# Attention of a hybrid decoder: eight heads per token tile, probabilities turned by VectorE in 32 by 32 blocks, values in 32-row products

## The chip, the cores and the metric

One NeuronCore of a Trainium2 chip, one launch of one program. The metric is the device time of the launch in microseconds. A run is timed several times; the profile is one further execution with its own time.

The engines are named as in the profile: PE is TensorE's matrix products and PEld its loading of weights, DVE is VectorE, ACT is ScalarE, POOL is GpSimd, SP is SyncE, which here only issues DMAs. In the code they are `T`, `V`, `A`, `G` and `nc.sync`.

## The reference

Two layers (DEPTH = 2) over 1024 tokens of width 1024, all in f32. A layer normalises x, modulates it, projects it to 3088 columns, runs three groups of heads beside each other, gates each and projects back:

```python
h = rms_norm(x, pre_gain) * (1.0 + scale) + shift
(aq, ak, av, ag, rq, rk, rv, rg, gq, gk, gv, gg, ga) = jnp.split(h @ w_in, IN_SPLITS, axis=-1)
a_out = sliding_window_attention(rotary(aq), rotary(ak), av, sinks) * silu(ag)   # 8 heads on 2 kv heads, width 64
r_out = rms_norm(retention(rotary(rq), rotary(rk), rv)) * silu(rg)               # 4 heads
g_out = rms_norm(gated_linear_attention(gq, gk, gv, log_a)) * silu(gg)           # GLA, 4 heads
y = concat([a_out, r_out, g_out]) @ w_out
x = x + gate * rms_norm(y, post_gain)
```

The change concerns the attention. Each of the eight token tiles of 128 tokens looks at itself and at the tile before it: key j of the two tiles is allowed for query i where 0 <= i + 128 - j < 128. So of the previous tile the keys after the query's own place are allowed, of the current tile those up to it: exactly 128 keys for each query, which together fill one 128 by 128 square. Four query heads share one key and value head. A learned sink per head adds one logit to the softmax, whose probability is dropped:

```python
s = einsum('bnqhgd,bnkhd->bnhgqk', qb, kk) * D ** -0.5          # kk: previous and current tile
s = where(valid, s, -1e30)
p = softmax(concatenate([s, sink], -1), -1)[..., :-1]
o = einsum('bnhgqk,bnkhd->bnqhgd', p, vv)
```

## The kernel before, in words

**Stages.** A layer (`layer`) runs: modulation and the normalised, transposed input; the projection of the gates of GLA and retention; retention; GLA (`do_gqk`, `do_gv`, job `gla_core`); keys and values of the attention (`do_kv`); its queries (`attn_rot`); the projection of the attention's gates (`project_T` with `ag0`, `ag1`, job `gate`); the output projection. In layer 1 the output projection forms sums and differences of token pairs first (`last_output`, `sw_first`, the input `w_last`). A projection product of f32 is made of three passes over a split into a high and a low part (`PASSES`, `split`), 24 products of 128 by 128 weights with 256 or 512 moving columns each; all products of `mult` stand at L165, all transposes of TensorE at L180, all copies of the helper `copy` at L149 (ACT) or beside it, all DMAs of the helper `dma` at L154.

**The order of PE.** PE's instructions run in the order in which the program emits them (`tc.manual_schedule` for PE alone). A planner writes this order while the program is built: `clk` adds up an assumed cost of every product; a job is a generator that emits some work and yields either a latency from the table `L` (`lat("aq3", l)`) or the name of a flag; `pump()` between two pieces of a projection resumes every job whose time has come, so its products stand between those of the projection. `await_flag` moves the clock forward to a flag. The other engines, and SP's DMA queue, are ordered by the framework around that. The table `EN` says which engine makes each copy or DMA.

**Memory.** PSUM has eight banks: three under `mm()` for the projections, five under `aux()` for everything else. SBUF tiles come from rotating tags: `t2` (512 columns, B2 = 10), `t1` (256 columns, B1 = 8), `smx` for the softmax (SMB = 3), `mx` (`mix_tile`) for mixed inputs of the output projection, which the attention uses for its queries as well.

**Attention.** `attn_kv(l, t, pk)` copies the values of a token tile to SBUF (tag `va`, eight of them), turns the keys by rotary and transposes them into `kT`, high and low. `attn_rot(l, hf, g, w_)` projects the queries of half hf (four token tiles) and head group g (four heads) transposed, so that head channels lie on partitions, applies rotary with tables loaded from DRAM (`tabS`), swaps row blocks by small DMAs (`qst`), and a job (`split_later`, L839) splits them into high and low. `attn_run` goes over halves, groups, token tiles and starts one job `attn_q` for each: 32 units over both layers. A unit of four heads:

- scores: twelve products (two pairs of heads, three passes, two row halves side by side) into two aux banks;
- out of PSUM into `smx` 128 x 4 x 129: the previous tile's scores by ACT (`sprev`), over them the current tile's allowed ones by DVE's masked copy (L920, mask `curmask`); the 129th column is the sink;
- softmax: maximum on DVE (L922), four exponentials with sums on ACT (L925), reciprocal on DVE (L928), scaling on POOL (L929);
- after the latency `aq3`: four transposes on PE (L180) into one aux bank, copied to SBUF by ACT (`pf0`); POOL keeps the causal part in a second tile `pr` (affine_select);
- after `aq4`: the values as two products over 128 keys, once all keys with the previous tile's values, once the causal part with the difference `vd = v[t] - v[t-1]` (POOL), each in two column halves, into one aux bank; ACT copies it out (`aoc`), a DMA stores it to `aoS` in DRAM.

`gate(g, hf, kk, pm)` waits for the flags of the four `attn_q` of its half and group, loads their rows from `aoS`, multiplies them by the gate (L1590 on DVE), splits and stores the result to `mixS` (layer 1: some to `mixF`). The output projection loads `mixS` by `load_mix`.

Emission order around it: `do_kv(0)`, `do_gv(3)`, `do_kv(1..3)`, `job(attn_run)`, then `attn_rot` for the two halves and two groups, then the gates of half 0 and half 1, then the output.

Other lines that the text names: L1099, L1120 and L1121 are in GLA (`gla_core`), L635 in the normalisation (`rstd_of`), L1248 in `finish`, L533 and L515 to L545 in the weight loader (`loader`, `convert`), L704 and L666 in `pre`.

## Time and profile before

| | us |
|---|---|
| median of 3 runs | 998.84 |
| lowest and highest | 996.67, 999.44 |
| the profiled execution, its own time | 996.31 |
| its span in the profile | 994.6 |

| engine | busy us | share of the span | instructions |
|---|---|---|---|
| PE | 965.7 | 97% | 7133 |
| DVE | 683.2 | 69% | 1679 |
| ACT | 409.3 | 41% | 1152 |
| POOL | 246.3 | 25% | 310 |

The mean granted TensorE clock of this execution is 0.991 of full speed. The profiled execution lies 2.5 us under the median and 0.4 us under the lowest of the timed runs.

How to read it: a row of groups names the line, the engine, the operation, output <- inputs with the tile names of the program, partitions x elements, the count, busy time and mean ns of one instruction, and behind the last bar the idle time of the engine just before them and what ended most of it. A row of a timeline has the start in us from the span's start, the duration, the engine and the operation; products that follow one another are one row. PE's products overlap, so a row's duration exceeds the distance to the next start. A chain row names what released the step after it.

### The profile page before, as it was taken

To read this page: it belongs to the slowest core of one execution; us is meant where nothing else is said; L and a number is where in the kernel's file an instruction comes from. 1 tells how busy PE (TensorE), PEld (TensorE's weight loads), DVE (VectorE), ACT (ScalarE), POOL (GpSimd) and SP (SyncE) were. 2 spreads that over 40 slices of the span, in tenths; PEclk is the share of its full clock that TensorE was granted. 3 is DMA by queue.
4 is the path that set the end of the run, shared out by engine and by line. 5 is a ranking of instruction groups with operands and counts; after the bars stand their busy time and mean duration, and the time that the engine had idled before them with its cause. 6 is when DMAs were issued, how large, how long until landed. Compare 5 with 4: busy or idle time off the path is not lost.

```text
span 994.6 us, 19641 instructions
## 1 busy us (share of the span) xinstructions
PE 965.7 (97%) x7133; PEld 824.3 (83%) x7133; DVE 683.2 (69%) x1679; ACT 409.3 (41%) x1152; POOL 246.3 (25%) x310
## 2 busy tenths in 40 slices
PE   5899999999999999999999999999999999999996
PEld 1599999888998777778889999988999877777785
DVE  3779857677766777664677286775766577567876
ACT  2477312233332656632555332133333257574222
POOL 2322001233310234420124101113322034545000
PEclk8899999999999999999999999999999999999999
DMA  9843513523135355587555241352122434378883
GB/s 321 290 138 97 159 44 115 177 86 121 61 100 166 91 157 168 170 274 239 189 170 171 69 150 38 118 157 83 53 93 86 127 91 133 112 235 266 267 262 139
DMA packets 112305, 148.77 MB, mean 150 GB/s; under 512 B 12065, under 2 KB 63821, under 8 KB 112209
## 3 DMA queue, kind: packets, MB, share of 16 engines
q1 hardware_dynamic: 106512, 137.96, 44.5%
q10 hardware_dynamic: 5696, 9.56, 2.6%
q8 instruction: 56, 0.92, 0.4%
q14 instruction: 41, 0.33, 0.1%
HBM read 109.20 MB, written 36.18 MB: 146 GB/s over the span
## 4 chain that ended last, share of the span: by engine, by line
PE 80%; DVE 7%; DMA 7%; issue 2%; POOL 1%; ACT 1%; SPq 0%; ACTq 0%; POOLq 0%; DVEq 0%
PE mm L165 61%; PE aux L165 14%; PE aux L180 5%; DMA st<-in_w_in_dram 2%; POOL sm L635 1%; DMA t<-aoS 1%; DMA st<-in_w_last_dram 1%; DMA xk<-in_x_dram 1%; DVE arena L533 1%; DMA a<-mixS 1%; DVE t L1248 0%; DVE t L328 0%; DMA t<-in_x_dram 0%; DMA t<-xs 0%; DMA mixS<-t 0%
## 5 line engine op out<-in xcount | busy, mean ns | idle before, releaser
L165 PE MATMUL mm<-arena 128*128 128x256 f32 (+2 forms) x1824 | 299.9, 318 | 1.8 <-ACT arena L704 1.8
L165 PE MATMUL mm<-arena,arena 128*128 128x256 f32 (+2 forms) x1824 | 298.2, 316 | 0.0
L165 PEld LDWEIGHTS mm<-arena 128*128 128x128 f32 x1824 | 255.5, 191 | 26.0 <-issue 3.3
L165 PEld LDWEIGHTS mm<-arena,arena 128*128 128x128 f32 x1824 | 252.2, 188 | 24.3 <-issue 3.7
L635 POOL TENSOR_TENSOR sm<-sm,mhalf 128x1 f32<-128x1 f32 (+1 forms) x64 | 55.8, 872 | 335.9 <-DVE sm L634 317.8
L165 PE MATMUL mm<-arena,mx 128*128 128x512 f32 (+1 forms) x564 | 130.6, 387 | 0.5 <-ACT kept L1341 0.5
L165 PEld LDWEIGHTS mm<-arena,mx 128*128 128x128 f32 x564 | 101.4, 188 | 24.7 <-issue 1.9
L149 ACT ACTIVATE t<-aux 128x256 f32<-128x256 f32 (+2 forms) x124 | 55.8, 468 | 73.8 <-PE aux L180 62.2
L149 ACT ACTIVATE arena<-st 128x512 fp32r<-128x512 f32 x94 | 56.2, 627 | 53.2 <-DMA st<-in_w_in_dram 19.4
L929 POOL TENSOR_TENSOR smx<-smx,sm 128x512 f32<-128x512 f32 x32 | 36.1, 1129 | 125.7 <-DVE sm L928 118.0
L533 POOL TENSOR_TENSOR arena<-st,arena 128x512 fp32r<-128x512 f32 x31 | 42.7, 1378 | 79.7 <-ACT arena L149 72.9
L533 DVE TENSOR_TENSOR arena<-st,arena 128x512 fp32r<-128x512 f32 x77 | 58.0, 775 | 5.2 <-ACT arena L149 3.3
L925 ACT ACTIVATE smx<-smx,sm 128x129 f32<-128x129 f32 x128 | 49.9, 393 | 25.9 <-DVE sm L922 25.7
L364 DVE SCALAR_TENSOR_TENSOR acc<-st,c_act,acc 128x512 f32<-128x512 f32 x60 | 46.7, 778 | 16.9 <-DMA st<-in_w_mod_dram 16.5
L180 PE MATMUL aux<-c_ident,t 128*128 128x128 f32 (+1 forms) x292 | 48.2, 282 | 5.4 <-DVE t L666 5.0
L180 PEld LDWEIGHTS aux<-c_ident,t 128*128 128x128 f32 (+1 forms) x292 | 35.0, 144 | 12.4 <-DVE t L666 6.9
L698 ACT ACTIVATE t<-aux,mod,mod 128x128 f32<-128x128 f32 x68 | 25.9, 459 | 43.0 <-DVE t L1248 18.1
L165 PEld LDWEIGHTS aux<-t,mx 32*128 32x128 f32 (+1 forms) x896 | 39.5, 187 | 3.9 <-issue 2.1
L973 ACT ACTIVATE t<-aux 128x256 f32<-128x256 f32 x32 | 12.3, 383 | 73.6 <-PE aux L165 65.0
L165 PE MATMUL aux<-t,mx 32*128 32x32 f32 (+1 forms) x896 | 40.7, 272 | 0.0
L920 DVE COPY_PREDICATED smx<-c_curmask,aux 128x256 f32<-128x256 int32 x64 | 25.4, 446 | 19.5 <-ACT smx L149 17.2
L1248 DVE SCALAR_TENSOR_TENSOR t<-t,sm,t 128x512 f32<-128x512 f32 x32 | 24.0, 780 | 18.2 <-DMA t<-in_x_dram 10.8
(224 smaller groups left out, 1387.7 us busy)
## 6 DMA issues: line engine op xcount, KB each, us to landing
st<-in_w_in_dram SPq DMA_DIRECT2D x96, 256.0 KB, 3.8
st<-in_w_mod_dram SPq DMA_DIRECT2D x64, 256.0 KB, 3.1
mx<-mixS SPq DMA_DIRECT2D x20, 512.0 KB, 4.9
mixS<-t SPq DMA_DIRECT2D x72, 128.0 KB, 3.7
st<-in_w_last_dram SPq DMA_DIRECT2D x36, 256.0 KB, 3.8
wm<-in_w_mod_dram SPq DMA_DIRECT2D x12, 512.0 KB, 7.0
t<-in_x_dram SPq DMA_DIRECT2D x24, 256.0 KB, 4.9
t<-tabS SPq DMA_DIRECT2D x16, 256.0 KB, 4.6
```

Source lines behind the costliest of these rows:

```text
L149: A.activation(dst, src, AF.Copy)
L165: T.matmul(dst, lhsT, rhs, start=start, stop=stop)
L180: T.transpose(dst, src, idn)
L364: V.scalar_tensor_tensor(acc, wt, c_act[:, k:k + 1], acc, ALU.mult, ALU.add)
L533: e.tensor_tensor(lo, st, f(hi), ALU.subtract)
L635: G.tensor_tensor(r, r, mhalf[:, :w], ALU.pow)
L698: A.activation(hf[:, ks], at[kt], AF.Identity, scale=gain, bias=shift)
L920: V.copy_predicated(sv, curmask.unsqueeze(1).to_broadcast((P, 2, P)), pv[:, :, n // P - 1, :])
L925: A.activation(sm[:, h, :], sm[:, h, :], AF.Exp, bias=mx[:, h:h + 1], accum_out=sums[:, h:h + 1])
L929: eng("pn").tensor_tensor(sm[:, :, 0:128], sm[:, :, 0:128], rs.unsqueeze(2).to_broadcast((P, 4, P)), ALU.mult)
L973: A.activation(sq, po, AF.Square)
L1248: V.scalar_tensor_tensor(xt[j], yg[j], r, xt[j], ALU.mult, ALU.add)
```

## The change

Attention is computed per token tile for all eight heads, in 16 units instead of 32.

- **Queries.** `attn_rot` keeps both groups of a half in one f32 `mx` tile; `attn_q` splits the 128 tokens it needs (`qs`, one buffer). The `tabS` loads are issued only after the copy of a given value tile (`kv["at"]`). `attn_rot` of half 0 and `job(attn_run)` now stand ahead of `do_kv(2)` and `do_kv(3)`.
- **Scores.** 24 products into four aux banks; four `sprev` copies and four masked copies; the softmax works on 128 x 8 x 129; POOL scales 128 x 8 x 128.
- **The turn.** No transposes on PE, no PSUM copy of them, no affine_select. DVE transposes the scaled probabilities in place in 32 by 32 blocks: block (i, j) of queries and keys stays in its place and is turned inside. So a partition block i of 32 rows then holds, for every key block j, the 32 keys of j on its partitions and the 32 queries of i as columns.
- **The causal part.** Only the diagonal blocks are mixed between the two tiles: `pr`, four POOL products of 32 partitions with a 32 by 32 mask (`dmask`).
- **Values.** They go to DRAM (`vS`), and `attn_v(p)` loads them for a pair of tiles with each 32-key block replicated on the four partition blocks (five DMAs). For partition block i and round s, key block (i + s) mod 4 uses the current tile's values below the diagonal and the previous tile's elsewhere; a last round adds `pr` with `vd`. That makes 40 products with 32 rows, 64 columns and 128 moving columns (20 for token tile 0), into four aux banks, one per partition block i. The copies out of them alternate between ACT (`aoc0`) and DVE (`aoc1`); one DMA stores the tile to `aoS`.
- **Order.** `attn_run` starts a unit only after the scores of the unit before (flag `sc`) and, from the fourth on, after the values three units back (flag `av`); `load_mix` waits for the scores of single tiles. Latencies: `aq1` 11, `aq2` 2.6, `aq4` 17, `aq6` 7.
- **Memory.** B1 = 7 instead of 8; `smx` tiles are twice as wide; the eight `va` tiles are gone; the scratch for dynamic DMAs is set to 1024.

The diff, cut to its core:

```diff
-    def split_later(mq, q, name):
...
     def attn_kv(l, t, pk):
         kr = t1()[:, 0:P]
-        v = kv["v"]
-        v[t] = gp.tile([P, P], F32, tag="va", name=nm("va"), bufs=VDB)
-        A.activation(v[t], pk[:, 128:256], AF.Copy)
+        v = t1()[:, 0:P]
+        i = A.activation(v, pk[:, 128:256], AF.Copy)
+        if t in (2, 6):
+            kv["at"] = i
+        dma("sv", vS[t], v)
...
+    def attn_v(p):
+
+        x = gp.tile([P, 10, P], F32, tag="vx", name=nm("vx"), bufs=2)
+        for i in range(4):
+            dma("lv", x[32 * i:32 * i + 32, 0:8], vS[2 * p:2 * p + 2].rearrange("t (j b) d -> b (t j) d", b=32))
+        dma("lv", x[:, 8:10], vS[2 * p:2 * p + 2].rearrange("t k d -> k t d"))
+        kv[("v", p)] = x
 
     def attn_run(l):
...
+        yield (0.0, ("kT", l, 3))
+        attn_v(0)
+        attn_v(1)
+        for t in range(NT):
+            yield (lat("aq1", l) if t else 0.0, ("q", l, t // 4, 1))
+            yield (0.0, ("kT", l, t))
+            if t:
+                yield (0.0, ("sc", l, t - 1))
+            if t >= SMB:
+                yield (0.0, ("av", l, t - SMB))
+            job(attn_q(l, t, kv[t // 4]))
+
+    def attn_q(l, t, q):
+
+        qs = gp.tile([P, 2, 4, P], F32R, tag="qs", name=nm("qs"), bufs=1)
+        split(qs[:, 0], qs[:, 1], q[:, :, P * (t % 4):P * (t % 4) + P])
+        sm = gp.tile([P, 8, 129], F32, tag="smx", name=nm("smx"), bufs=SMB)
...
+        yield lat("aq2", l)
+        pss = [[aux(), aux()], [aux(), aux()]]
...
-        eng("pn").tensor_tensor(sm[:, :, 0:128], sm[:, :, 0:128], rs.unsqueeze(2).to_broadcast((P, 4, P)), ALU.mult)
-        yield lat("aq3", l)
-
-        pp = aux()
-        for h in range(4):
-            transp(pp[:, h * P:(h + 1) * P], sm[:, h, 0:128], ident)
-        pf = t2()
-        copy("pf0", pf, pp)
...
+        ph = sm[:, :, 0:128]
+        eng("pn").tensor_tensor(ph, ph, rs.unsqueeze(2).to_broadcast((P, 8, P)), ALU.mult)
+        pb = ph.rearrange("p h (j b) -> p h j b", j=4)
+        V.transpose(pb, pb)
+        cur, prev = kv[("v", t // 2)], kv.get(("v", max(t - 1, 0) // 2))
+        tc_, tp = t % 2, (t - 1) % 2
         if t > 0:
-            pr = t2()
-            G.affine_select(h4(pr), h4(pf), [[0, 4], [1, P]], ALU.is_ge, 0.0, base=0, channel_multiplier=-1)
-            parts.append((vd, pr))
+            vd = gp.tile([P, P], F32, tag="vd", name=nm("vd"), bufs=1)
+            G.tensor_tensor(vd, cur[:, 8 + tc_], prev[:, 8 + tp], ALU.subtract)
+            pr = gp.tile([P, 8, 32], F32, tag="pr", name=nm("pr"), bufs=1)
+            for i in range(4):
+                rr = slice(32 * i, 32 * i + 32)
+                eng(f"pr{i}").tensor_tensor(pr[rr], pb[rr, :, i, :], dmask[rr].unsqueeze(1).to_broadcast((32, 8, 32)),
+                                            ALU.mult)
         yield lat("aq4", l)
-        po = aux()
...
+        po = [aux() for _ in range(4)]
+        for s in range(5 if t else 4):
+            for i in range(4):
+                rr = slice(32 * i, 32 * i + 32)
+                j = (i + s) % 4
+                if t == 0 and j > i:
+                    continue
+                for r in range(2):
+                    cc = slice(64 * r, 64 * r + 64)
+                    d3 = po[i][cc, 0:128].rearrange("p (h a) -> p h a", h=4)
+                    if s == 4:
+                        w_, x = vd[rr, cc], pr[rr, r:8:2, :]
+                    else:
+                        w_ = cur[rr, 4 * tc_ + j, cc] if j < i or t == 0 else prev[rr, 4 * tp + j, cc]
+                        x = pb[rr, r:8:2, j, :]
+                    mult(d3, w_, x, s == 0, s == (4 if t else -i % 4 if i < 2 else 3), 0.03)
+        ao = t2()
+        av = ao.rearrange("p (h q) -> p h q", h=4)
+        for i in range(4):
+            copy(f"aoc{i % 2}", av[:, :, 32 * i:32 * i + 32], po[i][:, 0:128].rearrange("p (h a) -> p h a", h=4))
+        flag(("av", l, t))
+        dma("sao", aoS[t], av)
...
+        if t in (2, 4):
+            attn_v(t // 2 + 1)
...
         do_gv(3)
-        for p in range(1, NP_):
+        do_kv(1)
+        for g in range(2):
+            attn_rot(l, 0, g, used(l, f"aq{g}"))
+            pump()
+        job(attn_run(l))
+        for p in range(2, NP_):
             do_kv(p)
...
-B2, B1, BS, BST, MMB, SMB = 10, 8, 11, 5, 3, 3
+B2, B1, BS, BST, MMB, SMB = 10, 7, 11, 5, 3, 3
```

More of the change, by code (lines that the diff above doesn't have):

```diff
@@ new lines, in attn_q @@
+        flag(("sc", l, t))
+        if t % 4 == 3:
+            flag(("s", l, t // 4))
+        for g in range(2):
+            for r in range(2):
+                pv = pss[g][r][:, 0:2 * n].rearrange("p (j c n) -> p j c n", j=2, n=P)
+                sv = sm[:, 4 * g + r:4 * g + 4:2, 0:128]
+                if t > 0:
+                    copy("sprev", sv, pv[:, :, 0, :])
+                V.copy_predicated(sv, curmask.unsqueeze(1).to_broadcast((P, 2, P)), pv[:, :, n // P - 1, :])
+        mx = small(8)
@@ L1678 @@
 CHUNK = 7
 LAG = 2
-VDB = 8
 FIN = 1
```

108 lines of the change are left out of this document (39 added, 69 removed).

## The prediction

> **What bounds the kernel now.** I read the page's shares first, then its chain, then stretches of the trace around attention.
>
> ```profile
> span 994.6 us, 19641 instructions
> PE 965.7 (97%) x7133; PEld 824.3 (83%) x7133; DVE 683.2 (69%) x1679; ACT 409.3 (41%) x1152; POOL 246.3 (25%) x310
> PE 80%; DVE 7%; DMA 7%; issue 2%; POOL 1%; ACT 1%; SPq 0%; ACTq 0%; POOLq 0%; DVEq 0%
> ```
>
> TensorE (PE) is busy 97% of the span and holds 80% of the chain that ended last: an instruction taken from PE is time won, as long as PE still finds its inputs ready. Attention (scores, softmax, values) lies in two stretches, one per layer, between the first and the last VectorE (DVE) masking of scores. The columns are the busy time of each engine:
>
> ```profile
> core 0: us, PE busy (x) PEld busy (x) DVE busy (x) ACT busy (x) POOL busy (x), PEclk, DMA share, GB/s
> 317.80:423.30 105.50, 105.50 (x645) 79.26 (x645) 76.72 (x149) 64.63 (x206) 39.22 (x44) 1.00 0.45 138
> 791.00:887.50 96.50, 96.50 (x594) 69.94 (x592) 66.78 (x133) 61.87 (x204) 40.83 (x44) 1.00 0.45 135
> ```
>
> PE has no hole in either, at full granted clock; DVE is busy 73% and 69% of them. So the question is whether DVE, already the second engine, still keeps up when these stretches get shorter for PE.
>
> **PE's part.** Rows of PE's timeline, start and duration; the price of a group is the distance to the next start:
>
> ```profile
> 336.79 0.39 PE L165 MATMUL mm<-arena,arena 128*128 128x512 f32 x1
> 337.02 0.60 PE L180 MATMUL aux<-c_ident,smx 128*128 128x128 f32 x4
> 337.37 1.19 PE L165 MATMUL mm<-arena,arena 128*128 128x512 f32 x4
> 338.49 0.98 PE L165 MATMUL aux<-kT,mx 64*128 64x256 f32 x12
> 339.40 0.65 PE L165 MATMUL aux<-t,va 128*64 128x256 f32 x4
> 339.98 2.35 PE L165 MATMUL mm<-arena,arena 128*128 128x512 f32 x9
> ...
> 355.09 0.65 PE L165 MATMUL aux<-t,va 128*64 128x256 f32 x4
> 355.57 0.60 PE L165 MATMUL aux<-t,vd 128*64 128x256 f32 x4
> 356.10 1.20 PE L165 MATMUL mm<-arena,arena 128*128 128x512 f32 x4
> ...
> 219.84 1.54 PE L165 MATMUL aux<-t,mx 32*128 32x32 f32 x48
> 221.20 0.40 PE L165 MATMUL aux<-t 32*128 32x32 f32 x8
> 221.53 0.75 PE L165 MATMUL mm<-arena 128*128 128x256 f32 x4
> ```
>
> For each token tile and group of four heads, PE now spends 0.35 us on four turns (337.02 to 337.37), 0.91 on twelve score products (338.49 to 339.40) and 1.01 on values (355.09 to 356.10; 0.58 at token tile 0, 339.40 to 339.98). Over 32 such units: 11.2 + 29.1 + 28 x 1.01 + 4 x 0.58 = 70.9 us.
>
> After, per token tile: the turns are gone. Scores are one run of 24 instead of two of 12. Twelve products take 0.91 us with the start of the run; six more pairs, at about 0.12 a pair, make 1.62. The values become 40 products of 32 rows by 64 columns with 128 moving columns (20 at tile 0), each two PE instructions, since the four of 355.09 are two products. The trace has no such shape. The old value run shows two column halves side by side: 4 instructions of 256 moving columns in 0.48 us are two rounds of 0.24, so a round of 128 columns is 0.12. Retention's neighbour, GLA, has 32-row products: 56 instructions in 1.69 us (219.84 to 221.53), 30 ns each, or 0.12 per round of four row groups. Lower bound: four row groups and two halves all together, 80 instructions in 10 rounds, 1.2 us. Upper bound: 30 ns each as in GLA, 2.4 us. I take 1.25, because both kinds of splitting appear separately. Sum: 16 x 1.62 + 14 x 1.25 + 2 x 0.7 = 44.8, so 26 us less. The runs also enter and leave the stream less often: four instructions from 337.37 to 338.49 take 1.12 against 4 x 0.235 elsewhere in the stream, so 0.1 to 0.2 is lost on a switch; 64 fewer runs at 0.1 give 6. PE's gain is 32 us; with the upper bound 14.
>
> The Trainium skill (TensorEngine Tiling (Array Packing), Instruction Overhead) charges about 60 cycles to every matmul, which would be an estimated 2 us for 80 instructions and 12 us less gain; GLA's 30 ns row would allow it, while the two halves at once speak against it.
>
> **What DVE gets, and in which order.** Groups by shape (busy, mean ns of one):
>
> ```profile
> L920 DVE COPY_PREDICATED smx<-c_curmask,aux 128x256 f32<-128x256 int32 x64 | 25.4, 446 | 19.5 <-ACT smx L149 17.2 <-PE aux L165 2.3
> L922 DVE TENSOR_REDUCE sm<-smx 128x4 f32<-128x516 f32 x32 | 21.9, 685 | 0.5
> L928 DVE RECIPROCAL sm<-sm 128x4 f32<-128x4 f32 x32 | 5.6, 174 | 17.2 <-ACT smx L925 17.1
> L929 POOL TENSOR_TENSOR smx<-smx,sm 128x512 f32<-128x512 f32 x32 | 36.1, 1129 | 125.7 <-DVE sm L928 118.0 <-DVE smx L897 4.4 <-DVE sm L279 3.2
> L839 DVE TENSOR_TENSOR mx<-t,mx 128x512 fp32r<-128x512 f32 x16 | 12.4, 812 | 1.2 <-ACT mx L838 1.2
> L1099 POOL TENSOR_TENSOR t<-t,gs 128x256 f32<-128x256 f32 x8 | 6.4, 795 | 0.0
> L1121 DVE COPY_PREDICATED mx<-c_mask,aux 128x128 f32<-128x128 int32 x64 | 14.3, 297 | 15.2 <-ACT mx L1120 15.2
> L1590 DVE SCALAR_TENSOR_TENSOR t<-t,t 128x512 f32<-128x512 f32 x16 | 11.6, 727 | 8.8 <-DMA t<-aoS 8.8
> ```
>
> ```profile
> 358.02 0.69 DVE L922 TENSOR_REDUCE sm<-smx 128x4 f32<-128x516 f32 x1
> 360.43 0.18 DVE L928 RECIPROCAL sm<-sm 128x4 f32<-128x4 f32 x1 [1.72 <-ACT smx L925]
> ```
>
> Eight heads in one piece lengthen the chain of one token tile, which runs over four engines. From the scores' end: four masked copies 1.6 (4 x 446 ns, overlapping a little), the split of the next queries 0.75 (L839, now placed here), a maximum twice as wide 1.25 (2 x 685), eight exponentials 3.4 (four take 1.72, from the wait of 360.43), reciprocal and hand-over 0.2, scaling on POOL 2.2 (2 x 1129), the new turn on DVE, then two of the four copies of the values of the previous tile, 0.5 (L1121's shape, 297 each). The turn moves 1024 elements per partition; the maximum's rate gives 1.3, twice that is the upper bound, half of it the lower; I take 1.1. That sums to 11.0 us. On POOL, pr (four times about 0.6, bounds 0.3 and L1099's 0.8) follows the turn; only the last eight of 40 products need it, and 5 us or more of projection stand before the values, so it costs nothing. The removed PSUM copy (ACT) and causal selection (POOL), the added value loads (SP; tokens stored a tile earlier) and kT's work lie beside PE and count zero; if the loads came late, vd and the values would wait a landing, some 5 us. One buffer fewer in t1, and rotary begun earlier beside GLA: 0 to 4 us, I take 0 since no PE hole of the earlier stages names them.
>
> The compiled order of DVE decides. For token tiles 2 to 7 it puts the turn of tile t ahead of the copies of tile t-1's values out of PSUM. Scores and values each take four of the five aux banks, so the second half of scores t+1 waits for those copies, and they for the whole chain of tile t. PE plans 12 to 13 us from one score run to the next (8 to the last), DVE 11.0 plus what is queued between: weight splits, gate products, rotary, at 0.6 to 0.8 each. And in-order waits: after the maximum DVE stands up to 3.4 us, after the reciprocal 2.2, unless other work is put there.
>
> The worst place is tile 5. Between its masked copies stand two gate products L1590, which wait for attention rows of tiles 0 to 3 stored and loaded back; tile 3's copies are the last of it:
>
> ```profile
> 914.70 2.52 DMA aoS<-t
> 917.24 0.02 SPq L154
> 917.26 0.03 issue
> 917.29 4.30 DMA t<-aoS
> 921.59 0.02 issue
> 921.61 0.69 DVE t L1590
> ```
>
> Store and load take 2.52 + 4.30 = 6.9 us, and tile 3's copies end only about when scores 5 start. So those products start 7 us after scores 5 began instead of 1.7; then two of them 1.3, two masked copies 0.8, one more 0.7, maximum 1.2, exponentials 3.4, 0.2, POOL 2.2, the turn 1.2, copies with a cast between 0.8: 18.8 us after scores 5, where PE planned the second half of scores 6 at 12.7. That is 6 us of hole. Tile 6 starts its masked copies 3.5 us later still (split results of the gate), needs 11, and scores 7 follow scores 6 in 8 us: another 6.5. Tile 3, behind five rotary products and a weight split, loses 5.8 and tile 5's own scores 2.3. Layer 0: about 20; layer 1, where w_last's differences stand in the same places, the same way: 20. Bounds: only the two structural losses, 11.0 + 0.9 against 8 at scores 7 and half of tile 5's, 6 a layer; or all of it and the slower turn, 1.2 more in six rounds, 28.
>
> At the end, the four gate pieces of tokens 4 to 7 now all hang on one last value run, PE has 20 us of products before it needs tile 3's rows from mixS, and those loads stand in SP's queue behind the pieces' stores:
>
> ```profile
> 933.60 3.50 DMA t<-xs
> 937.10 0.02 issue
> 937.12 0.02 SPq L154
> 937.13 0.03 issue
> 937.16 7.31 DMA a<-mixS
> 944.48 0.14 issue
> 944.61 5.55 PE mm L165 x23
> ```
>
> Copy 0.6, store 2.5, load 4.3 to 6, four gate pieces 5, store 3.5, load 7.3: 24 us, 4 more than PE's cover. Bounds 0 and 10.
>
> **Sum.** -32 + 40 + 4 = +12 us. The profiled execution took 994.6 us of span and 1.7 around it, 996.3; so 1008.3. The median of the runs, 998.84, lies 2.5 higher; on its footing 1011.
>
> **Rivals.**
> 1. Faster. The score banks are freed in time because rotary and gate products really stand where DVE waits anyhow: then only the structural 6 a layer and the end remain, -32 + 12 + 4 = -16, 983. For it: PE has no hole today, with the same DVE work at 73%. Against: the bank order above. With half the holes it is -32 + 20 + 4 = -8, 991; this is the likelier of this kind. The point from which it decides: holes under 28 us in all.
> 2. No change: 26 to 30 us of holes, DVE paying back PE's gain almost exactly; 996 to 1002. The Trainium skill (TensorEngine Tiling (Array Packing), PSUM Bottleneck) speaks against the change in this way: packing speeds the products, not the emptying of PSUM, so a gain there may be lost whole. No row of before shows it, since PE has no hole.
> 3. Slower still: the value products run at 30 ns each. PE gains 14, though part of that lies in holes that stand anyway; with two thirds of the 18 lost, 1023; with the slower turn as well, 1033.
>
> **How the numbers follow.** Measurement tells 0.3% apart, 3 us. Forecast (holes outweigh the gain) 0.52; rival 3 0.13; rival 2 0.09; rival 1 0.26. So slower 0.65, same 0.09, faster 0.26. The range leaves out the upper end of rival 3 and the best of rival 1: 987 to 1031; the forecast's own is 1003 to 1022.
>
> **What would show it.** After, the value runs should take 1.2 to 1.4 us (2.4 with rival 3), the turn 1.1; PE's holes should stand before score runs, released by DVE's or ACT's copies of values out of aux, largest before the scores of tiles 3, 6 and 7; DVE should be at or above 80% between the first and the last masked copy, in stretches of about 105 us rather than 88. Wrong if PE stays without holes there, if the copies of values precede the turn, or if holes stand elsewhere: at the value runs (chain too long), at the projections (rotary's PSUM), or in the gates of other stages (one t1 buffer fewer).

## The result and the profile after

The changed kernel takes 1057.62 us (median of 4 runs, 1054.20 to 1061.39) against 997.75 us of the kernel before: a ratio of 1.060, 95% interval 1.055 to 1.065. It is slower, as forecast, but by 60 us, not 12, and outside the range of 987 to 1031. The profiled execution took 1055.40 us with a span of 1053.6, 59.0 more than before. Line numbers have moved: products are now L166, the copies of the helper L150 (ACT) and L152 (DVE), the mask copies L935, the gate product L1627 (L1590 before).

The page's first lines and the view of cores, after:

```profile
span 1053.6 us, 21257 instructions
PE 968.1 (92%) x7965; PEld 837.9 (80%) x7965; DVE 703.8 (67%) x1679; ACT 386.0 (37%) x1120; POOL 259.7 (25%) x306
```

```profile
core 0: 1053.6 us, clock 0.959
```

PE is busy as long as before (968.1 against 965.7 us) although it has less to do, and its mean granted clock is 0.959 where it was 0.991. So the 59 us have two parts: time in which PE does nothing, and time in which it works at a lower clock.

Where, by stage: both kernels cut at the same places among the projection products (GLA, attention, output and next layer's input; then layer 1's GLA, attention and the rest; the row between the layers, 164.7 us before and 164.1 after, is left out). Columns as in the prediction: busy time of PE, PEld, DVE, ACT, POOL, then the granted clock. Before:

```profile
205.20:296.00 90.80, 90.21 (x1059) 83.77 (x1058) 66.27 (x212) 31.85 (x101) 28.07 (x42) 1.00 0.31 97
296.00:437.80 141.80, 141.80 (x823) 107.32 (x821) 101.58 (x195) 74.49 (x235) 45.41 (x50) 1.00 0.53 160
437.80:533.80 96.00, 95.86 (x507) 80.42 (x506) 59.82 (x138) 42.76 (x118) 17.65 (x24) 1.00 0.66 217
...
698.50:760.90 62.40, 62.24 (x771) 58.06 (x770) 43.81 (x146) 22.52 (x76) 19.63 (x28) 1.00 0.29 90
760.90:893.10 132.20, 132.20 (x798) 100.26 (x797) 88.84 (x187) 71.93 (x232) 45.73 (x49) 1.00 0.43 129
893.10:994.60 101.50, 91.53 (x417) 72.05 (x415) 73.96 (x129) 32.41 (x77) 19.52 (x19) 0.98 0.74 234
```

After:

```profile
206.50:313.90 107.40, 102.51 (x1059) 91.65 (x1058) 71.10 (x208) 30.84 (x97) 26.43 (x40) 0.98 0.40 118
313.90:451.70 137.80, 123.17 (x1167) 99.53 (x1166) 100.00 (x187) 62.61 (x220) 50.78 (x50) 0.96 0.47 145
451.70:561.10 109.40, 100.34 (x578) 84.09 (x577) 67.00 (x151) 43.06 (x120) 18.69 (x26) 0.95 0.63 207
...
725.20:800.50 75.30, 72.06 (x782) 66.48 (x781) 45.75 (x148) 23.45 (x77) 19.48 (x27) 0.91 0.31 95
800.50:922.80 122.30, 113.93 (x970) 92.83 (x968) 79.83 (x156) 53.27 (x179) 40.87 (x37) 0.97 0.41 121
922.80:1053.60 130.80, 103.55 (x650) 81.54 (x648) 89.54 (x158) 39.32 (x110) 32.35 (x31) 0.88 0.65 211
```

GLA and attention of layer 0 together take 245.2 us instead of 232.6 (rotary has moved from the second row into the first), the output and next input 109.4 instead of 96.0; in layer 1 it is 197.6 instead of 194.6, and the rest 130.8 instead of 101.5. Attention's last units slip behind the cuts: layer 1's last row after holds one score run and three value runs, with waits of 8.4 us. In each row shown after the clock is below 1.00.

What PE waited for (total us, times, longest), before and after:

```profile
PE aux L180 <- DVE t L666: 5.0, 3, 3.2
PE aux L165 <- ACT t L149: 3.0, 3, 1.3
...
PE mm L165 <- DMA a<-mixS: 1.5, 1, 1.5
...
PE aux L180 <- DVE mx L1121: 0.2, 1, 0.2
```

```profile
PE aux L166 <- DVE t L152: 15.8, 7, 4.4
PE aux L166 <- ACT t L150: 15.0, 6, 6.9
PE aux L181 <- DVE t L669: 14.4, 5, 5.3
PE mm L166 <- DVE t L1378: 6.7, 3, 5.0
...
PE aux L181 <- DVE mx L1154: 5.1, 4, 2.0
PE mm L166 <- DVE t L1340: 4.2, 2, 3.8
PE aux L166 <- DVE smx L935: 3.2, 2, 2.2
```

The first two rows after are waits for copies out of aux. Of their 30.8 us, 27.9 stand at score runs, which wait for copies of values, where nothing was; the rest lies in retention, like the 3.0 before. Of the 14.4 us for L669 (normalised input), 5.5 lie in the first 50 us, like the 5.0 at L666 before; 8.9 lie behind layer 0's attention, and L1378 and L1340 (last output) lie behind layer 1's: 19.8 us together, against 2.0 before. L1154 is GLA, where the new waits are 7.6 us in all. L935 are value runs: a mask copy empties a score bank of the next tile, and the value run writes to that bank next. So the new waits are 27.9 us at score runs, 3.2 at value runs, 17.8 behind attention and 7.6 in GLA. (The expectations below speak of 31 us at score runs and 34 or 35 with the value runs; those figures hold retention's 3 us as well.)

**The clock.** The largest waits are of this kind (after, all engines; tile 7's scores stand for the copies of tile 5's values):

```profile
426.67 1.19 PE L166 MATMUL aux<-smx,vx 32*64 32x128 f32 x62
...
428.05 0.38 PE L166 MATMUL aux<-kT,qs 64*128 64x256 f32 x1
428.52 0.40 ACT L940 ACTIVATE smx<-smx,sm 128x129 f32<-128x129 f32 x1 [0.30 <-DVE sm L937]
...
432.10 0.42 ACT L150 ACTIVATE t<-aux 128x128 f32<-128x128 f32 x2
...
432.41 1.64 PE L166 MATMUL aux<-kT,qs 64*128 64x256 f32 x11 [3.98 <-ACT t L150]
```

ACT makes eight exponentials of tile 6 first; PE stands for 3.98 us. And then the granted clock (the number before the last two) in stretches of 1 us:

```profile
431.00:432.00 1.00, 0.00 (x0) 0.00 (x0) 0.20 (x1) 1.00 (x5) 0.00 (x0) 1.00 1.02 277
432.00:433.00 1.00, 0.59 (x5) 0.59 (x6) 0.69 (x1) 0.52 (x3) 0.90 (x1) 0.52 0.62 123
...
437.00:438.00 1.00, 1.00 (x6) 0.76 (x3) 0.32 (x1) 0.67 (x2) 0.93 (x2) 0.50 0.97 369
...
439.00:440.00 1.00, 1.00 (x6) 0.82 (x5) 0.72 (x1) 0.24 (x1) 0.00 (x0) 1.00 0.52 193
```

For 6.8 us behind the wait PE runs at half clock. In the clock's records such stretches add up to 87.7 us, 19.2 before. Less the waits inside them (13.9 and 2.8), half of what is left is put down as lost: 36.9 us, 8.2 before. About 3 us of either figure, and of each in the table below, belong to a stretch behind PE's last product, where nothing is lost; the difference hardly changes by it (28.7, or 28.6 without). The gaps of more than 0.3 us between products add up to 71.0 us, 14.4 before. So the 59.0 us are +56.6 of gaps, +28.7 of clock, and the remainder, -26.3, is put down to PE's gain.

**The prices of the new pieces**, by PE's timeline (distance to the next start) and by groups:

```profile
353.34 1.68 PE L166 MATMUL aux<-kT,qs 64*128 64x256 f32 x24
354.96 1.21 PE L166 MATMUL mm<-arena,arena 128*128 128x512 f32 x4
...
444.63 1.19 PE L166 MATMUL aux<-smx,vx 32*64 32x128 f32 x62
...
446.00 1.20 PE L166 MATMUL mm<-arena,mx 128*128 128x512 f32 x4
```

```profile
L956 POOL TENSOR_TENSOR pr<-smx,c_dmask 32x256 f32<-32x256 f32 x56 | 45.3, 809 | 12.2 <-DVE smx L947 4.5 <-DVE smx L912 4.5
...
L945 POOL TENSOR_TENSOR smx<-smx,sm 128x1024 f32<-128x1024 f32 x16 | 31.2, 1949 | 98.7 <-DVE sm L943 85.8 <-DVE sm L292 6.5 <-DVE sm L282 6.4
...
L947 DVE STREAM_TRANSPOSE smx<-smx 128x1024 f32<-128x1024 f32 x16 | 19.8, 1240 | 10.1 <-POOL smx L945 10.1
```

A score run is 1.62 us, a value run 1.37 (1.10 at tile 0), the turn 1.24, scaling 1.95, one diagonal product 0.81.

### The profile page after: what moved, and what is told of

The parts are those of the page before. It is cut to its first block, busy times and chain, and to the rows that moved or that the text cites. A ratio compares the mean times of both kernels' runs of the same rounds, so it can differ in the third digit from the quotient of the medians.

```text
span 1053.6 us, 21257 instructions
## 1 busy us (share of the span) xinstructions
PE 968.1 (92%) x7965; PEld 837.9 (80%) x7965; DVE 703.8 (67%) x1679; ACT 386.0 (37%) x1120; POOL 259.7 (25%) x306
## 5 line engine op out<-in xcount | busy, mean ns | idle before, releaser
L166 PE MATMUL mm<-arena 128*128 128x256 f32 (+2 forms) x1824 | 303.3, 323 | 2.1 <-ACT arena L707 1.8
L166 PE MATMUL mm<-arena,arena 128*128 128x256 f32 (+2 forms) x1824 | 296.6, 317 | 0.0
L166 PEld LDWEIGHTS mm<-arena 128*128 128x128 f32 x1824 | 262.3, 195 | 26.4 <-ACT arena L707 2.0
L166 PEld LDWEIGHTS mm<-arena,arena 128*128 128x128 f32 x1824 | 254.7, 190 | 23.6 <-issue 1.8
L166 PE MATMUL mm<-arena,mx 128*128 128x512 f32 (+1 forms) x564 | 137.3, 402 | 6.7 <-DVE t L1378 6.7
L166 PEld LDWEIGHTS mm<-arena,mx 128*128 128x128 f32 x564 | 106.7, 197 | 32.4 <-DVE t L1378 5.4
L150 ACT ACTIVATE arena<-st 128x512 fp32r<-128x512 f32 x94 | 56.1, 628 | 78.6 <-PE mm L166 40.5
L181 PE MATMUL aux<-c_ident,t 128*128 128x128 f32 (+1 forms) x292 | 50.0, 290 | 22.2 <-DVE t L669 14.4
L181 PEld LDWEIGHTS aux<-c_ident,t 128*128 128x128 f32 (+1 forms) x292 | 35.8, 147 | 30.6 <-DVE t L669 11.0
L166 PE MATMUL aux<-kT,qs 64*128 64x256 f32 (+1 forms) x384 | 33.6, 311 | 27.9 <-DVE t L152 15.8
L150 ACT ACTIVATE t<-aux 128x128 f32<-128x128 f32 (+3 forms) x92 | 32.4, 379 | 70.5 <-PE aux L181 51.5
L367 DVE SCALAR_TENSOR_TENSOR acc<-st,c_act,acc 128x512 f32<-128x512 f32 x60 | 45.5, 758 | 15.4 <-DMA st<-in_w_mod_dram 14.8
L166 PEld LDWEIGHTS aux<-kT,qs 64*128 64x128 f32 x384 | 27.7, 204 | 35.2 <-DVE t L152 17.4
L945 POOL TENSOR_TENSOR smx<-smx,sm 128x1024 f32<-128x1024 f32 x16 | 31.2, 1949 | 98.7 <-DVE sm L943 85.8
L956 POOL TENSOR_TENSOR pr<-smx,c_dmask 32x256 f32<-32x256 f32 x56 | 45.3, 809 | 12.2 <-DVE smx L947 4.5
L166 PEld LDWEIGHTS aux<-t,mx 32*128 32x128 f32 (+1 forms) x896 | 40.9, 194 | 4.0 <-issue 3.0
L166 PE MATMUL aux<-t,mx 32*128 32x32 f32 (+1 forms) x896 | 42.1, 279 | 0.0
L1281 DVE SCALAR_TENSOR_TENSOR t<-t,sm,t 128x512 f32<-128x512 f32 x32 | 24.2, 781 | 26.6 <-DMA t<-in_x_dram 15.0
```

The costliest lines, as they stand in the source:

```text
L150: A.activation(dst, src, AF.Copy)
L166: T.matmul(dst, lhsT, rhs, start=start, stop=stop)
L181: T.transpose(dst, src, idn)
L367: V.scalar_tensor_tensor(acc, wt, c_act[:, k:k + 1], acc, ALU.mult, ALU.add)
L945: eng("pn").tensor_tensor(ph, ph, rs.unsqueeze(2).to_broadcast((P, 8, P)), ALU.mult)
L956: eng(f"pr{i}").tensor_tensor(pr[rr], pb[rr, :, i, :], dmask[rr].unsqueeze(1).to_broadcast((32, 8, 32)), ALU.mult)
```

## The experiments

Gaps and clock loss are worked out as above, from each run's profiled execution; 997 is the kernel before.

| run | median us | gaps | lost by clock |
|---|---|---|---|
| before | 997 | 14.4 | 8.2 |
| after | 1057.6 | 71.0 | 36.9 |
| e1_order | 1055.7 | 70.3 | 36.8 |
| e2_rot | 1069.8 | 76.2 | 43.0 |
| e3_gate | 1053.4 | 68.0 | 41.7 |
| e4_hole | 1039.9 | 38.8 | 29.2 |
| e5_split | 1057.1 | 60.8 | 41.8 |
| e6_gate | 1048.5 | 63.9 | 38.5 |
| e7_copies | 1055.4 | 70.9 | 30.0 |
| e8_b1 | 1000.6 | 12.9 | 12.1 |
| e9_noturn | 1052.3 | 68.5 | 35.6 |
| e10_halves | 1058.4 | 69.3 | 41.3 |
| e11_banks | 1071.5 | 86.3 | 34.9 |
| e12_nosoft | 1038.4 | 58.6 | 32.4 |
| e13_nosoft_gate | 1029.1 | 51.1 | 30.6 |
| e14_mix | 1047.5 | 59.1 | 41.3 |
| e15_gates | 1036.0 | 55.2 | 34.0 |
| e16_gates_nosoft | 1013.3 | 45.1 | 26.6 |
| e17_mix | 1051.3 | 61.0 | 38.4 |

### What a wait costs PE: e4_hole

```diff
+    def hole(n):                        # called in retention behind token pairs 0 to 2
+        pa = aux(); transp(pa[:, 0:P], ident, ident)
+        x = t2(); G.memset(x[:, P:512], 0.0); V.tensor_copy(x[:, 0:P], pa[:, 0:P])
+        for _ in range(n): G.tensor_tensor(x, x, x, ALU.add)
+        pb = aux(); transp(pb[:, 0:P], x[:, 0:P], ident); V.tensor_copy(small(8), pb[:, 0:8])
+HOLE = (1, 4)                            # n for layer 0, layer 1
```

> The kernel before, with six waits put into PE's stream in retention, three short ones in layer 0 (one POOL addition on the way, about 2.5 us) and three long ones in layer 1 (four POOL additions, about 6 us); no packed product is in it. If a long hole itself halves the clock behind it, each long one is followed by 3.4 to 6.8 us at half clock (1.7 to 3.4 us lost), and the time is 1027 to 1040 us. Rival (the lower clock in the changed kernel belongs to its 32-row products): no stretch at half clock, and the time is 997 plus the holes, about 1022.

1039.9 us, the upper end of the theory's range: 43 us more than before, for waits that the view of waits puts at 24.3 us in all:

```profile
PE aux L180 <- POOL t L961: 24.3, 6, 6.6
```

One of them in the timeline, and the stretches around it:

```profile
616.25 0.47 PE L180 MATMUL aux<-c_ident,t 128*128 128x128 f32 x1 [4.92 <-POOL t L961]
```

```profile
612.00:617.00 5.00, 0.75 (x4) 0.75 (x5) 0.17 (x1) 0.00 (x0) 3.96 (x4) 0.84 0.19 64
617.00:624.00 7.00, 7.00 (x41) 6.71 (x41) 1.30 (x5) 1.07 (x3) 0.19 (x1) 0.63 0.04 7
624.00:631.00 7.00, 7.00 (x62) 7.00 (x61) 5.92 (x19) 3.44 (x5) 1.44 (x2) 1.00 0.04 14
```

Behind the waits of 4.92, 5.21 and 6.56 us stand 6.8, 6.8 and 10.2 us at half clock, behind those of 3.53 and 2.13 us 3.4 each, behind 1.96 none. None of the changed kernel's 32-row value products is in this kernel: the wait itself brings the lower clock. The stretches right behind the waits lose 11.5 us. Two further ones in GLA, of 13.7 and 3.4 us, followed gaps of 1.69 and 0.56 us and lose another 8.5; they are part of the 43. The Trainium skill (TensorE: Matmul & The Clock Gate, "What's actually happening") says that PE falls to half clock after about one idle window of 3.4 us and needs about as long a busy one to come back: the lengths agree, in steps of 3.4 us, but a wait of 2.13 us was enough here.

### Undoing the order that the forecast blamed: e1_order, e7_copies, e9_noturn

```diff
+        if t: yield (0.0, ("av", l, t - 1))
+        with tc.issue_after(<last copy of tile t-1's values on VectorE>):
             V.reciprocal(rs, sums)
...
+        with tc.issue_after(<the same>):
             V.transpose(pb, pb)
```

> The changed kernel, with one thing moved: on VectorE the reciprocal and the turn of token tile t are queued behind the two copies of tile t-1's values out of PSUM. Theory of the forecast (the score runs wait for copies that stand behind the turn in VectorE's order): of the 31 us that PE waits at score runs for copies out of aux, at least 15 go, and with them half of the stretches at half clock in attention; 1020 to 1040 us. Rival (VectorE has simply too much work per tile, whatever the order, and the later turn makes the values late): the waits move to the value runs, and the time stays within 1050 to 1065 us.

1055.7 us: no difference. At score runs the waits for DVE's copies fell from 15.8 to 7.1 us, those for ACT's rose from 12.1 to 14.8; behind attention those for L670, the normalised input, rose from 8.9 to 11.0. The time is the rival's, but the value runs hardly wait more (4.7 us against 3.2).

e7_copies is the same with `"aoc0": "V"`.

> The kernel with the turn behind the copies of the tile before, and all four copies of the values on VectorE, none on ACT. If the score runs now wait mostly for ACT's copies, which stand behind eight exponentials (17 us there), these waits go and 10 to 20 us with their clock: 1030 to 1045. Rival (VectorE's own queue is the limit): VectorE's copies take over the waits, 1050 to 1065.

1055.4 us: the rival. The waits at score runs are now for DVE's copies alone, 21.8 us. DVE around the largest of them in layer 0 (the products of tile 5's values ended at 426):

```profile
427.56 0.68 DVE L1632 SCALAR_TENSOR_TENSOR t<-t,mm 128x512 f32<-128x512 f32 x1
430.78 0.69 DVE L1632 SCALAR_TENSOR_TENSOR t<-t,mm 128x512 f32<-128x512 f32 x1 [2.54 <-ACT t L1631]
431.38 0.17 DVE L918 COPY smx<-sink 128x8 f32<-128x8 f32 x1
431.45 0.88 DVE L153 COPY t<-aux 128x128 f32<-128x128 f32 x4
```

The copies are now ahead of the turn, but behind a gate's product that waits for ACT's tanh, which stands behind the eight exponentials.

e9_noturn leaves `V.transpose(pb, pb)` out.

> The changed kernel without VectorE's turn (the probabilities go unturned into the value products, so the output is not the reference's); every other instruction stays. If the pace of attention is VectorE's queue, 16 turns of 1.24 us and the waits for POOL ahead of them (7 us a layer) come out of the holes, with their clock: 1020 to 1038 us. Rival (the turn lies beside other work, the pace is set by other waits in the queues of VectorE and ACT): less than 8 us goes, 1047 or more.

1052.3 us, ratio 1.055 (1.053 to 1.058): the rival. The turn itself costs about 5 us.

### Other single links: e5_split, e10_halves, e11_banks

```diff
+            if g == 0:                   # between the two runs of 12 score products
+                yield 5.0
```

> The changed kernel, with the 24 score products of a token tile put into PE's order as two runs of 12, 5 us of other products or more apart; nothing else moves on purpose (the latency to the values is cut by the same 5 us). Theory (the score runs stand because four banks are asked for at once while the values of the tile before still hold them): of the 31 us of waits at score runs less than 12 stay, the stretches at half clock in attention go with them, 1010 to 1030 us. Rival (ACT, VectorE and POOL are too slow per tile, whatever the banks): the waits move to the value runs and the time stays at 1045 to 1060.

1057.1 us: the rival's time. The score waits fell to 7.9 us, but the value runs now wait 20.4 us (3.2 before the edit), and 17.5 of them end with mask copies (L937), not with late probabilities. One of them:

```profile
399.20 0.47 PE L166 MATMUL aux<-smx,vx 32*64 32x128 f32 x12
402.96 1.57 PE L166 MATMUL aux<-smx,vx 32*64 32x128 f32 x50 [3.29 <-DVE smx L937]
```

The turn of this tile ended at 393.3. Twelve instructions fill three banks; then PE stands until DVE's mask copies have emptied the fourth, which holds scores of the next tile. So banks were still what PE waited for, now in the other direction.

e10_halves makes maximum, exponentials, reciprocal, scaling and turn for four heads behind each run of 12.

> The changed kernel with scores in two runs of 12, and maximum, exponentials, reciprocal, scaling and turn done for four heads at a time behind each; mask products and values stay for all eight. If the pace is the long in-order chain (VectorE stands while ACT makes eight exponentials and while POOL scales), half of it now overlaps the other half, and the waits of 35 us at scores and values fall under 15: 1015 to 1040. Rival (the sum of VectorE's and ACT's work in these stretches sets it): 1045 to 1065, since it is a little more work.

1058.4 us: the rival. The value runs wait 28.9 us, 26.3 of them for mask copies again.

e11_banks is `MMB` 2 instead of 3.

> The changed kernel with one PSUM bank moved from the projections to the rest (2 and 6 instead of 3 and 5). If the score runs stand for a bank, 31 us of waits there fall under 15, less what projections lose by one bank: 1025 to 1048. Rival (a bank more only moves the wait to the next unit, since the copies come at the same pace): 1050 to 1075.

1071.5 us: the rival. The score waits stay at 26.5 us, and projections wait for DVE to empty their two banks.

### Rotary's place and the t1 buffer: e2_rot, e8_b1

```diff
-        do_kv(1)
-        for g in range(2): attn_rot(l, 0, g, ...)
-        job(attn_run(l))
-        for p in range(2, NP_): do_kv(p)
+        for p in range(1, NP_): do_kv(p)
+        job(attn_run(l))
+        for g in range(2): attn_rot(l, 0, g, ...)
```

> The changed kernel with the old place of the queries: rotary of half 0 and the start of attention behind all keys and values again. If the waits of PE in GLA (7 us more than before, and about 8 us lost to a lower clock there) come from rotary work that VectorE now does between GLA's own, they vanish, and the time falls by 8 to 15 us, to 1040 to 1048. Rival: they come from one t1 buffer fewer or from the stores of v; then GLA's stretches stay as they are and the time does not fall.

1069.8 us: slower than the changed kernel, and GLA's waits (L1154, 5.1 us) are unchanged. Three stretches at half clock in GLA stay too. The old place costs 12 us more; attention's last value run starts 14 us later in layer 0 and 17 in layer 1.

e8_b1 is the kernel before with `B1` 7.

> The kernel before with one buffer fewer in t1 (7 instead of 8), nothing else. If that buffer makes the waits in GLA of the changed kernel (about 7 us, with 8 us of lower clock), they appear here too: 1005 to 1013 us. Rival: they come from the attention's change; then no difference, 995 to 999.

1000.6 us, ratio 1.003 (1.001 to 1.005): between the two. The buffer costs about 3 us. Of GLA's waits it brings 1.5 us at L1105 (1.4 at the same line, L1138, in the changed kernel) and 0.6 at L1121, and two short stretches at half clock. The stores of v, which e2_rot's rival names beside the buffer, were not tried alone.

### The gates: e3_gate, e6_gate

```diff
-            dma("lao", ..., rows(aoS, hf, k))
+            dma("lao", ..., rows(aoS, 0, k))
```

> The changed kernel, but the gates of tokens 4 to 7 read the attention rows of tokens 0 to 3, which are long stored (so the output of half 1 is not the reference's); all work stays. If the waits behind attention (PE for the normalised input of layer 1, 5.3 and 3.6 us, and in the last output projection 1.4, 5.0 and 3.8 us) come from the four gate pieces that hang on the last value run's store and load, most of these 19 us go, and 4 to 8 us of lower clock behind them: 1028 to 1040. Rival: those waits come from VectorE's backlog or the DMA queue alone; then less than 5 us goes.

1053.4 us: the rival. The loads kept their place in SP's queue behind the last values' store, so the pieces still came together.

```diff
-            for t in range(4 * hf, 4 * hf + 4):          # e6_gate: and not planned behind
+            for t in range(4):                           # the last values either
                 yield (0.0, ("ao", l, t, g))
```

> The changed kernel, but the gates of tokens 4 to 7 neither read the rows of tokens 4 to 7 nor are put behind their values in the order of emission: they use those of tokens 0 to 3 (half 1 of the attention's output is not the reference's). If the pile of four gate pieces behind the last value run makes the waits after attention (about 19 us in both layers, and 9 us of clock behind them), these go and the time is 1028 to 1040. Rival (VectorE's backlog out of attention does it): less than 8 us goes, 1046 or more.

1048.5 us: 9 us less than the changed kernel, hardly more than the rival's 8. In the last output projection the waits for L1378 fell from 6.7 to 2.0 us and those for L1340 went: layer 1's part of the pile is real. In layer 0 the wait of 5.3 us for L669 went, but tile 7's score waits grew from 5.5 to 10.3 us: there the waits only moved.

### Taking away whole parts: e12_nosoft, e13_nosoft_gate, e15_gates, e16_gates_nosoft

```diff
-        V.tensor_reduce(mx, sm, ...) ... A.activation(... Exp ...) ... V.reciprocal(rs, sums)
-        eng("pn").tensor_tensor(ph, ph, rs..., ALU.mult)
-        V.transpose(pb, pb)
-            eng(f"pr{i}").tensor_tensor(pr[rr], ...)
-            G.memset(sm[:, :, 0:128], -1e30)       # token tile 0
+            G.memset(sm[:, :, 0:128], 0.0)
+                        w_, x = vd[rr, cc], pb[rr, r:8:2, i, :]
```

> The changed kernel with the softmax left out: no maximum, exponentials, reciprocal, scaling, turn and diagonal products; raw scores go into the value products (the output is not the reference's). All products of PE, their order, the copies out of PSUM, the stores and the gates stay. If the chain through VectorE, ACT and POOL between scores and values holds PE up, the 34 us of waits at scores and values and the 13 us of clock behind them go: 1000 to 1020. Rival (the products themselves, or PE's order, make the kernel slower): 1040 or more.

1038.4 us, ratio 1.041 (1.037 to 1.044), between theory and rival: the whole softmax holds 19 us. The waits at score runs fall from 27.9 to 9.3 us, those behind attention do not (23.4 after 19.8). What remains looks like this on DVE, at tile 5 (L1612 is the gate's product):

```profile
399.60 0.79 DVE L935 COPY_PREDICATED smx<-c_curmask,aux 128x256 f32<-128x256 int32 x2
405.72 0.69 DVE L1612 SCALAR_TENSOR_TENSOR t<-t,t 128x512 f32<-128x512 f32 x1 [5.33 <-DMA t<-aoS]
406.33 0.78 DVE L935 COPY_PREDICATED smx<-c_curmask,aux 128x256 f32<-128x256 int32 x2
```

The product waits 5.33 us for rows that were stored and loaded, and the second half of tile 5's mask copies waits behind it: the place the prediction called the worst.

e13_nosoft_gate is this with e6_gate's edit.

> As the run without softmax, and the gates of tokens 4 to 7 read the rows of tokens 0 to 3 and are not put behind the last values. If the rest of the loss after attention is the pile of gates, another 10 to 25 us go: 980 to 1003, so at or under the kernel before. Rival: less than 5 us below the run without softmax.

1029.1 us, ratio 1.032: 9 us less, as e6_gate had it, so under the step that was expected.

e15_gates lets all gates multiply rows of x, with no flag to wait for:

```diff
-            for t in range(4 * hf, 4 * hf + 4): yield (0.0, ("ao", l, t, g))
-            dma("lao", ..., rows(aoS, hf, k))
+            dma("lao", ..., x_in[0, 512 * hf:512 * hf + 512, P * k:P * k + P].rearrange("(t p) q -> p t q", p=P))
```

> The changed kernel, but all gates multiply rows of x in place of attention's rows, load them at once and wait for no values (the output is not the reference's); softmax, values and their stores stay. If the gates' round trip (store, load, the product waiting in VectorE's queue ahead of the next tile's work) is the larger part of the loss, 20 us or more go: 1020 to 1035. Rival (the softmax chain is the larger part, and the gates only the 9 us behind the last values): 1042 to 1052.

1036.0 us, ratio 1.039 (1.035 to 1.042): 1 us above the theory's range, and 22 us less, as it asked. The gates' wait for attention's rows holds a little more than the softmax. Here the waits behind attention fall from 19.8 to 3.6 us, while those at score runs stay (28.3 us).

> The same without the softmax too. If softmax chain and gates together make all waits of PE in and after attention, what is left of the loss is GLA's 7 us of waits and its clock, against 26 to 28 us less work on PE: 985 to 1000. Rival (something else in the change holds PE up as well): 1010 or more.

1013.3 us, ratio 1.015 (1.012 to 1.018): 44 us less than the changed kernel; 19 and 22 alone add up to 41. But it is the rival's side: the kernel is still slower than before, and score runs wait 16.1 us for the copies of values. PE and DVE at the largest of these waits in layer 0:

```profile
427.97 0.97 PE L166 MATMUL aux<-kT,qs 64*128 64x256 f32 x12 [3.09 <-DVE t L152]
426.57 0.69 DVE L1610 SCALAR_TENSOR_TENSOR t<-t,t 128x512 f32<-128x512 f32 x1 [1.10 <-DMA t<-in_x_dram]
427.64 0.28 DVE L152 COPY t<-aux 128x128 f32<-128x128 f32 x1
```

The gates' products (L1610) wait for their rows of x here, 29.9 us over the run, where in e15_gates none waits, and the copies of values stand behind them. So this edit did not take away all of the gates' waiting: the rows need no value run now, but their loads still come after DVE is ready for them.

### Versions: e14_mix, e17_mix

e14_mix adds to e7_copies:

```diff
+            with tc.issue_after(<newest maximum on VectorE>):
                 V.scalar_tensor_tensor(ao, th, 0.5, ao, ALU.mult, ALU.mult)
-            if t >= SMB:
-                yield (0.0, ("av", l, t - SMB))
+            if t >= 2:
+                yield (0.0, ("av", l, t - 2))
+                yield 2.0
```

> The changed kernel with three edits of order at once: all copies of values on VectorE and the turn behind them, the gate products queued on VectorE behind the newest maximum (not ahead of the next tile's mask copies), and the score run of tile t at least 2 us of plan behind the values of tile t-2. If the in-order queue of VectorE with the gates in it is what keeps single edits from showing: 1015 to 1040. Rival (the length of the softmax chain itself, whatever the order): 1045 to 1060.

1047.5 us, ratio 1.050 (1.047 to 1.053): 10 us less than the changed kernel, the fastest of the versions that leave nothing out; in the rival's range. One wait of 8.5 us is left at tile 6 of layer 1, where DVE stands 5.16 us for a piece of `w_last` and then has a queue before the copies.

> The run with three edits of order (1047.5 us), and the gate products of half 0 planned 9 us later still. If gate products ahead of attention's own in VectorE's queue still cost there: 1030 to 1042. Rival (they are already out of the way): 1043 to 1052.

1051.3 us: the rival. No version beat the kernel before.

## Why the prediction was wrong

Its direction holds, and so does its mechanism for about half of the new waits: PE's gain is lost to waits at score runs, behind copies that come late out of in-order queues. But by its own signs it was wrong too, since waits also stand at value runs, in GLA and, far more than it gave them, behind attention. Its sum was -32 + 40 + 4 = +12: PE's gain, score banks, the end. Measured are -26.3 for PE's gain, 31.1 at score and value banks, 17.8 behind attention, 7.6 in GLA and 28.7 by the clock, together +59.

1. **A term was missing: the clock, +29.** The sum priced each wait at its own length. The kernel before has no wait of over 1.5 us after its first 50 us, so its rows show full clock, and the prediction quoted that clock without asking what waits would do to it. e4_hole shows that waits alone do it: 24 us of them made that kernel 43 us slower. This is the step that failed first and by most; at the changed kernel's own rate, 28.7 on 56.6, the forecast's 44 us of waits would have cost an estimated 66, and the sum would have been +34.
2. **Waits at score banks, +40: the size was near, the cause too narrow.** Measured are 27.9, and 3.2 at value runs, largest at tiles 3 and 7 of layer 1 and at tile 7 of layer 0; tile 5's mask copies did stand behind gate products. But "the compiled order of DVE decides", with the turn ahead of the copies, is refuted: with the order mended (e1_order, e7_copies), or without the turn (e9_noturn), other work in the queues of DVE and ACT held the copies. So it is partly luck that the size came near. Taken away whole, the softmax is worth 19 us, mostly by the score runs' waits, and the gates' wait for attention's rows 22, mostly by the waits behind attention.
3. **The end, +4 (0 to 10): 17.8.** The pile of gate pieces was seen, for layer 1 only. Both layers have it: of the 19.8 us there, 8.9 are behind layer 0's attention (L669) and 10.9 behind layer 1's (L1378, L1340). They nearly go (3.6 us) when the gates need no attention rows (e15_gates); e6_gate puts what the pile of half 1 costs at 9 us.
4. **Counted at nothing: GLA.** Given 0 to 4 us, it has 7.6 us of new waits, 4.9 of them at L1154, and three stretches at half clock, which lose 8 us. Not rotary's place (e2_rot), and only partly the t1 buffer (e8_b1). DVE's order in GLA differs from before; why is open, and the stores of v were not tried alone.
5. **PE's gain, -32: -26.** Score runs 1.62 as forecast. Value runs 1.37 against 1.25, and 1.10 against 0.7 at tile 0: the runs sum to 14 x 1.62 + 2 x 1.49 + 14 x 1.37 + 2 x 1.10 = 47.0 instead of 44.8 (1.49 is the score run at tile 0). That is 24 us less than 70.9; the fewer switches, put at 6, are left with the other 2, which no run measures alone. The 80 instructions take 17 ns each, so rival 3 (30 ns) is out; by the forecast's own terms it would have cost 17 us of the gain, not 18, since two of the 16 runs are half as long. The 60-cycle charge that the Trainium skill (TensorEngine Tiling (Array Packing), Instruction Overhead) names gave an estimated 2 us a run (and 11 us less gain, not 12, for the same reason); the measured 1.37 us does not bear it out. The Trainium skill (TensorEngine Tiling (Array Packing), PSUM Bottleneck) says that packing does not speed the emptying of PSUM; the 31.1 us of waits at banks agree.
6. **DVE's chain, 11.0.** From the end of tile 2's scores (355.0) to the end of its turn (369.3) are 14.4 us, where the forecast had 10.5 (11.0 less the copies of values behind it). The pieces had the forecast's sizes (turn 1.24 for 1.1, scaling 1.95 for 2.2), the rest is other work in between. The four diagonal products on POOL are 3.2 us instead of 2.4. DVE is busy 76% and 73% from first to last mask copy, not 80% or more, in stretches of 112 and 115 us.

Open: what changed DVE's order in GLA, and how much would be left with softmax and gates both really out of the way, since e16_gates_nosoft still waits for the gates' loads.

## What to carry to other kernels

Price a wait on PE at its length and the half-clock stretch behind it, and ask for each new wait how much of it can fall into one clock window (below); a kernel whose PE never stands shows nothing of this in its profile. Where a unit of work crosses three in-order engines, count all that those queues hold, not the one instruction that the change puts ahead of another: here, mending one link moved the wait to the next, run after run. A saving on the bound engine is only worth what the work beside it can follow, and taking away whole parts showed that sooner than reordering did.

## What the runs showed of the hardware

Four 32-row groups and two 64-column halves run side by side: 80 instructions with 128 moving columns in 1.37 us.

In all 19 traces PE's granted clock changes only at the borders of windows of 3.41 us, on one grid per trace. In a window at full clock, what counted was the time without products. Windows with more than 1.88 us of it, 153 over all traces, were without exception followed by half clock. Of 3693 with less than 1.5 us, outside the first 60 us and GLA (205 to 315 and 695 to 810 us), three were. So it matters where a wait falls: one of 2.13 us in e4_hole lay in one window and was followed by 3.4 us at half clock, while one of 1.96 us there (1.24 and 0.72) and one of 2.54 us in the changed kernel (1.67 and 0.87) lay across a border and were not. From this, a wait of 3.8 us or more would always cost clock, an estimate: across one border, half of it, 1.9 us, still falls into one window. The waits of 4.9 to 6.6 us in e4_hole were followed by 6.8 to 10.2 us. In GLA less was enough: the changed kernel's windows there had 0.8 to 2.0 us without products, and most of their products were 32 by 32.

A 32 by 32 block transpose of 1024 f32 columns took 1.24 us on VectorE, as long as a maximum over 1032 (1.22).
